# Six of eight output chunks run in pairs, half of their steps with seven block products in place of eight

## The chip, the cores and the metric

The kernel runs on one core of one Trainium2 chip. The metric is device time in microseconds (us) of one execution, the median of three runs. In what follows PE is TensorE with its matmuls, PEld its weight loads (they overlap the matmuls), DVE is VectorE, ACT is ScalarE, POOL is GpSimd and SP the engine that issues the DMAs.

## The reference

One decoder layer with 256 tokens and a width of 4096, all in float32:

```python
proj = einsum('btd,dn->btn', x, w_in)            # 4096 x 12336
q, k_c, v_c, k_s, v_s, k_w, v_w, gates, z_nsa, u, v, z_gm, q_m, z_m = split(proj)
y_nsa = _nsa(q, ..., gates) * silu(z_nsa)        # 16 heads, three branches
y_gm  = _gmlp(u, v, ...) * silu(z_gm)
y_mem = _mem_xattn(q_m, mem, w_mem_kv) * silu(z_m)
h = einsum('btn,nd->btd', concatenate([y_nsa, y_gm, y_mem]), w_out)   # 4096 x 4096
x = layernorm(alpha * x + h, ln_g, ln_b)
```

The change is in the product with `w_out`: 256 rows of y, 4096 deep, 4096 columns.

## The kernel before, in words

**Two-part operands.** PE multiplies float32r operands of 12 significant bits, so every float32 operand is split in two by `split_from` (L184): ACT copies it to a float32r tile (the high half, L185), and DVE subtracts that from the source (the rest, L186). `product3` (L188) then makes three matmuls of 128x128 by 128x512 for one block product: high by rest (L190), rest by high (L191), high by high (L192). The y side is split once; each block of w_out (128 rows by 512 columns) is split when it is needed.

**Chunks and steps.** A chunk is 512 columns of a weight matrix. The eight chunks of `w_out`, `out0` to `out7`, come last. A chunk has 16 steps; a step (`KG = 2`) loads 256 rows of the chunk as one DMA of 512 KB (`load`, three steps ahead, four buffers), splits its two blocks of 128 rows, and multiplies each with both blocks of 128 tokens: 2 x 2 x 3 = 12 matmuls. Two PSUM banks hold a chunk's sums, one for each block of tokens (`c.acc`); five banks are in a ring for this ("acc") and three serve all else ("sd").

**Order.** The program order of each engine is the order of the code. In a step, DVE and ACT split the next step's first block, PE takes this step's first block, and so for the second one. A split has four buffers for its high halves and four for its rests, so ACT starts the high half of a block when PE is done with the block that is four earlier. Work that is not a large product is queued with a delay in steps (`later`), and done by `run_side` at the end of a step.

**What follows a chunk.** `done_out` adds the residual to both sums (`residual`, L794, from PSUM), takes their statistics (L795), and multiplies by the norm's g (L799), spread over three steps of the next chunk. `load_gb` prepares g and b for the final norm in `out2` and `out3`. The last chunk runs its first block of tokens six steps ahead (`LEAD`), and is followed by the norm and the stores.

Of the kernel before, what the change touches and what calls it, by code (L numbers as in the profile page):

```python
# [15 lines left out]
P = 128  # L16
# [34 lines left out]
def decoder_layer(ctx: ExitStack, tc: tile.TileContext, x, mem, w_in, w_cmp_k1, w_cmp_k2, w_cmp_v1,  # L51
# [53 lines left out]
    def warm_up(n):  # L105
        """The tensor engine's clock is at its full rate only after some microseconds of work."""
# [8 lines left out]
    # distance of a query to a key over 256 keys, for the second block of queries; the first  # L115
    # block's is its right half
# [24 lines left out]
    # adds the rows (part, group, chunk) of both parts: chunk j for the first half of block j, and  # L141
    # chunk j + 1 for the second
# [8 lines left out]
    def load_small():  # L151
        """Weights of little size, and their transposes."""
# [29 lines left out]
    # A float32 is the exact sum of its rounding to 12 significant bits and of the rest, which has  # L182
    # 12 bits at most: both are float32r operands of the tensor engine.
# [4 lines left out]
    def product3(out, w, m, start, stop):  # L188
        """w.T @ m of two-part operands, without the product of the two rests (below 2^-24)."""
# [69 lines left out]
    def buffer_T(name):  # L259
        """sums() into one buffer [128, 4, tokens]."""  # L260
# [8 lines left out]
    # -- what becomes of each chunk's result  # L269
# [23 lines left out]
    def add_z(col, dst, name):  # L293
        """z * sigmoid(z) into dst()."""
# [26 lines left out]
    def gated(ps, z, dst, lo_dst, name):  # L321
        """ps * z, in two parts."""
# [16 lines left out]
    def mem_attention(j):  # L339
        """Heads 2j and 2j+1 over the memory tokens."""  # L340
# [154 lines left out]
    # -- keys and values of the selected and the window branch  # L495
# [8 lines left out]
    def keys_cs():  # L504
        """Keys of the groups, transposed: compressed (after a column that is left out), selected."""
# [153 lines left out]
    # -- spatial gating  # L659
# [112 lines left out]
    def load_gb(s):  # L772
        """Rows g, g, b in two parts, the first on partitions 0-2 and the second on 32-34."""
# [16 lines left out]
    def residual(n, i, acc):  # L790
        if n % 4 == 0:
            res[2 * i + n // 4] = page(F32, f"res{i}_{n}")
        r = res_of(i, n)
        nc.vector.scalar_tensor_tensor(r, xr[n][:, i, :], ALPHA, acc, op0=OP.mult, op1=OP.add)  # L794
        nc.vector.bn_stats(fst[:, i, n, :], r)  # L795
# [68 lines left out]
    for n in range(8):  # L864
# [3 lines left out]
    LEAD = 6                    # steps of the last chunk that its first block of tokens is ahead  # L868
# [3 lines left out]
    tail = nsteps - NS          # the first step of the last chunk  # L872
    raw, parts = {}, {}

    def load(i, pieces=1):
        if i >= nsteps:
            return
        c, k = steps[i]
        t = wp.tile([P, KG, 512], F32, name="w", tag="w", bufs=4)
        r0 = c.order[k] * P  # L880
        src = c.w[r0:r0 + KG * P, c.col:c.col + c.width].rearrange("(k p) n -> p k n", p=P)
        for q in range(pieces):
            ks = slice(q * KG // pieces, (q + 1) * KG // pieces)
            nc.sync.dma_start(t[:, ks, :c.width], src[:, ks])
        raw[i] = t

    def split(i, j):
        """The two parts of a step's j-th block of rows."""
        if i >= nsteps:
            return  # L890
        c = steps[i][0]
        kind = "wppywpps"[(i - tail) % 8] if i >= tail else "w"
# [12 lines left out]
        split_from(raw[i][:, j, :c.width], hi[:, :c.width], lo[:, :c.width])  # L905
# [5 lines left out]
    def products_T(i, half):  # L911
        """Blocks 2 * half and 2 * half + 1 of the result's rows."""
# [31 lines left out]
    # prologue  # L944
# [4 lines left out]
    load(0, 2)  # L949
    nc.sync.dma_start(mnat[0][:, :, 256:512], rows0[:, :, 256:512])  # L950
    load(1)
    mnat[1] = load_rows(mem2, 1, "mn")
    load(2)
# [7 lines left out]
    for i in range(tail):  # L961
        now[0] = i
# [4 lines left out]
        load(i + 3)  # L967
        if i < 16 and i % 2 == 0 and i // 2 + 2 < 8:
            mnat[i // 2 + 2] = load_rows(mem2, i // 2 + 2, "mn")
        if c.name.startswith("out") and k == 12:  # L970
# [96 lines left out]
```

## Time and profile before

| | |
|---|---|
| Median of three runs | 1740.77 us (1740.71 to 1741.45) |
| The profiled execution, first to last instruction | 1740.7 us |
| PE busy | 1730.2 us, 99% |
| DVE busy | 1031.7 us, 59% |
| ACT busy | 858.2 us, 49% |
| DMA | 329.03 MB, mean 189 GB/s |
| Mean granted clock of PE | 0.998 |

The profiled execution's span and the median of the runs are the same to 0.1 us, so a sum made against the span stands against the median as well. Durations of matmuls overlap in the records, so the time from one start to the next is what counts for PE.

### The profile page before, as it was taken

What the parts mean: (1) busy time and instruction counts of PE and PEld (TensorE: products, weight loads), DVE (VectorE), ACT (ScalarE), POOL (GpSimd) and SP (SyncE); (2) the same over time, 40 slices, a digit from 0 to 9 for tenths busy, and PEclk for the clock granted to TensorE, in tenths of its full rate; (3) what the DMA queues carried; (4) which work ended last, traced back from release to release, by engine and by line L of the source; (5) the groups of instructions that cost most, each with busy time, mean ns of one, the idle gap of its engine ahead of it and who ended that gap; (6) DMA issues with size and microseconds to landing.
All of it is one profiled execution on the core that took longest, in us unless ns stands there. A gap on an engine that the chain in (4) does not pass through costs nothing.

```text
span 1740.7 us, 24856 instructions
## 1 busy us (share of the span) xinstructions
PE 1730.2 (99%) x9011; PEld 1471.6 (85%) x9011; DVE 1031.7 (59%) x1797; ACT 858.2 (49%) x1592; POOL 6.6 (0%) x18
## 2 busy tenths in 40 slices
PE   9999999999999999999999999999999999999998
PEld 7888888888888899888888888888888888888885
DVE  5555645555665555456676565766655555665565
ACT  4445545454554445445555455655444444554451
POOL 0000000000000000000000000000000000000000
PEclk9999999999999999999999999999999999999999
DMA  7666766655665657665555555556666666666673
GB/s 259 199 186 222 227 187 185 190 158 158 219 215 148 192 165 211 187 184 158 167 158 167 160 147 172 166 169 193 177 193 189 204 210 213 209 214 213 212 230 146
DMA packets 174763, 329.03 MB, mean 189 GB/s; under 512 B 10465, under 2 KB 20005, under 8 KB 174629
## 3 DMA queue, kind: packets, MB, share of 16 engines
q1 hardware_dynamic: 174640, 327.46, 62.6%
q8 instruction: 70, 1.15, 0.3%
q14 instruction: 53, 0.43, 0.1%
HBM read 323.23 MB, written 4.19 MB: 188 GB/s over the span
## 4 chain that ended last, share of the span: by engine, by line
PE 60%; DVE 0%; DVEq 0%; issue 0%; ACT 0%
PE acc L922 13%; PE acc L190 12%; PE acc L192 12%; PE acc L191 12%; PE acc L923 7%; PE ps_pt L631 1%; PE ps_s L584 1%; PE ps_o L190 1%; PE ps_o L192 0%; PE acc L925 0%; PE ps_o L191 0%; PE ps_w L585 0%; DVE res L834 0%; PE ps_s L585 0%; PE ps_ln L830 0%; PE ps_sv L702 0%
## 5 line engine op out<-in xcount | busy, mean ns | idle before, releaser
L186 DVE TENSOR_TENSOR wl<-w,wh 128x512 fp32r<-128x512 f32 (+1 forms) x1160 | 759.6, 677 | 645.8 <-ACT wh L185 639.6
L185 ACT ACTIVATE wh<-w 128x512 fp32r<-128x512 f32 (+1 forms) x1160 | 687.4, 617 | 786.4 <-PE acc L922 362.1
L922 PE MATMUL acc<-x,wh 128*128 128x512 f32 x1984 | 709.6, 400 | 0.5 <-DVE gates L528 0.5
L923 PE MATMUL acc<-x,wl 128*128 128x256 f32 x2048 | 563.3, 280 | 0.1
L922 PEld LDWEIGHTS acc<-x,wh 128*128 128x128 f32 x1984 | 372.8, 188 | 87.6 <-ACT wh L185 2.2
L923 PEld LDWEIGHTS acc<-x,wl 128*128 128x128 f32 x2048 | 386.6, 189 | 7.2 <-DVE wl L186 0.8
L190 PE MATMUL acc<-wl,x 128*128 128x512 f32 (+1 forms) x576 | 215.0, 373 | 0.0
L191 PE MATMUL acc<-wh,x 128*128 128x512 f32 (+1 forms) x576 | 211.8, 368 | 0.0
L192 PE MATMUL acc<-wh,x 128*128 128x512 f32 (+1 forms) x576 | 211.5, 367 | 0.0
L190 PEld LDWEIGHTS acc<-wl,x 128*128 128x128 f32 x576 | 108.2, 188 | 18.1 <-issue 0.9
L192 PEld LDWEIGHTS acc<-wh,x 128*128 128x128 f32 x576 | 108.2, 188 | 17.8
L191 PEld LDWEIGHTS acc<-wh,x 128*128 128x128 f32 x576 | 108.2, 188 | 17.1
L922 PE MATMUL acc<-mem,wh 128*128 128x512 f32 x248 | 90.6, 407 | 0.7 <-DVE mem L186 0.5
L190 PE MATMUL acc<-wl,y_nsa 128*128 128x512 f32 x232 | 90.3, 389 | 0.0
L192 PE MATMUL acc<-wh,y_nsa 128*128 128x512 f32 x232 | 90.3, 389 | 0.0
L191 PE MATMUL acc<-wh,y_nsa 128*128 128x512 f32 x232 | 90.3, 389 | 0.0
L923 PE MATMUL acc<-mem,wl 128*128 128x256 f32 x256 | 71.2, 283 | 0.0
L922 PEld LDWEIGHTS acc<-mem,wh 128*128 128x128 f32 x248 | 47.5, 192 | 12.5 <-DVE mem L186 0.8
L191 PEld LDWEIGHTS acc<-wh,y_nsa 128*128 128x128 f32 x232 | 43.6, 188 | 9.2
L192 PEld LDWEIGHTS acc<-wh,y_nsa 128*128 128x128 f32 x232 | 43.6, 188 | 9.1
L190 PEld LDWEIGHTS acc<-wl,y_nsa 128*128 128x128 f32 x232 | 43.6, 188 | 9.0
L190 PE MATMUL acc<-wl,mem 128*128 128x512 f32 x128 | 51.1, 399 | 0.0
(248 smaller groups left out, 1558.7 us busy)
## 6 DMA issues: line engine op xcount, KB each, us to landing
w<-in_w_in_dram SPq DMA_DIRECT2D x368, 512.0 KB, 3.6
w<-in_w_out_dram SPq DMA_DIRECT2D x128, 512.0 KB, 4.0
w<-in_w_mem_kv_dram SPq DMA_DIRECT2D x63, 512.0 KB, 4.8
w<-in_w_in_dram SPq DMA_DIRECT2D x32, 280.0 KB, 3.2
xn<-in_x_dram SPq DMA_DIRECT2D x8, 512.0 KB, 5.2
xr<-in_x_dram SPq DMA_DIRECT2D x8, 512.0 KB, 5.7
out_dram<-res SPq DMA_DIRECT2D x16, 256.0 KB, 2.0
mn<-in_mem_dram SPq DMA_DIRECT2D x7, 512.0 KB, 5.0
```

Of the source, the lines that this page charges most:

```text
L185: nc.scalar.activation(hi, src, AF.Copy)
L186: nc.vector.tensor_tensor(lo, src, hi.bitcast(F32), op=OP.subtract)
L190: nc.tensor.matmul(out, w[0], m[1], start=start, stop=False)
L191: nc.tensor.matmul(out, w[1], m[0], start=False, stop=False)
L192: nc.tensor.matmul(out, w[0], m[0], start=False, stop=stop)
L584: nc.tensor.matmul(ps[:, :k0], q, keys_cs()[:, g, 1:16 + nk], start=True, stop=True)
L631: nc.tensor.transpose(ps[:n, h * P:(h + 1) * P], src, ident)
L922: nc.tensor.matmul(c.acc[b], hi, x, start=(k + j == 0), stop=False)
L923: nc.tensor.matmul(c.acc[b][:, :SEQ], lo, x[:, :SEQ], start=False, stop=False)
```

## The change

Chunks 0 to 5 of `w_out` run as three pairs (chunks 0 and 1, 2 and 3, 4 and 5); chunks 6 and 7 run as before, after them. Within a pair, a step q covers 256 rows of `w_out` and the columns of both chunks: four blocks of weights B11, B21 (first chunk) and B12, B22 (second chunk), where the first digit is the block of rows; and four blocks A of y, where the first digit is the block of tokens. `KINDS` says how each of the 16 steps runs.

* A step of kind C makes the eight plain block products, 24 matmuls, from four split blocks of weights.
* A step of kind S makes seven block products, 21 matmuls. Its seven operands on the weights' side ("forms") are B11, B21, B22 and four sums: T1 = B12 - B11, T2 = B22 - T1, T3 = B22 - B12, T4 = B21 - T2. Each sum is a DVE operation on 128x512, and is then split by ACT and DVE as a block is. On y's side there are four sums too (`make_sforms`); they are made in the first pair for each of the eight S steps, kept, and used again by the other pairs.

A pair uses all eight PSUM banks, which hold the products P1 to P8; `end_pair` forms the four results from them. There are six buffers for split forms, and `make_form` runs four forms ahead of `use_form`. `load_gb` moves to chunk 6. The core of the diff:

```diff
-    for n in range(8):
+    for n in (6, 7):
         add(w_out, 512 * n, 512, yp, done_out(n), f"out{n}", y_order)
...
+    NPAIR = 3
+    KINDS = "CSCSCSCSCSCSCSSC"
...
+    def make_sforms(q):
...
+        a11, a21, a12, a22 = full[:, 0, :P], full[:, 0, P:], full[:, 1, :P], full[:, 1, P:]
+        nc.vector.tensor_tensor(full, y[:, :, 0].bitcast(F32), y[:, :, 1].bitcast(F32), op=OP.add)
+        nc.vector.tensor_tensor(t[:, 0], a21, a22, op=OP.add)
+        nc.vector.tensor_tensor(t[:, 2], a11, a21, op=OP.subtract)
+        nc.vector.tensor_tensor(t[:, 1], t[:, 0], a11, op=OP.subtract)
+        nc.vector.tensor_tensor(t[:, 3], a12, t[:, 1], op=OP.subtract)
+        split_from(t, sforms[q][:, :, 0], sforms[q][:, :, 1])
...
+            if KINDS[q] == "C":
+                f = [("B11", [("P2", "A11"), ("P4", "A21")]), ("B21", [("P2", "A12"), ("P4", "A22")]),
+                     ("B12", [("P3", "A11"), ("P8", "A21")]), ("B22", [("P3", "A12"), ("P8", "A22")])]
+            else:
+                f = [("B11", [("P1", "A11")]), ("B21", [("P2", "A12")]), ("T1", [("P5", "S1")]),
+                     ("B22", [("P3", "S4")]), ("T2", [("P6", "S2")]), ("T3", [("P7", "S3")]), ("T4", [("P4", "A22")])]
...
+        if j == 0:
+            load_to(min(pbase[s] + 6, len(loads)))
...
+        def summed(a, b2):
+            t = work.tile([P, 512], F32, name="wsum", tag="sm", bufs=5)
+            nc.vector.tensor_tensor(t, a, b2, op=OP.subtract)
+            return t
+        if name[0] == "B":
+            src = b(name)
+        elif name == "T1":
+            src = sums["T1"] = summed(b("B12"), b("B11"))
+        elif name == "T2":
+            src = sums["T2"] = summed(b("B22"), sums["T1"])
+        elif name == "T3":
+            src = summed(b("B22"), b("B12"))
+        else:
+            src = summed(b("B21"), sums["T2"])
+        made[i] = form_slot()
+        split_from(src, *made[i])
...
+        elif what == 1:
+            residual_sum(n0, 0, bk("P2"))
+            residual_sum(n0, 1, bk("P4"))
...
+        elif what == 3:
+            r = res_of(0, n0)
+            nc.vector.tensor_tensor(r, r, sums["U"], op=OP.add)
+            nc.vector.tensor_tensor(sums["U"], sums["U"], bk("P6"), op=OP.add)
...
+    FLEAD = 4
...
+            if m == 0 and j == 0 and q + 1 < NS and KINDS[q + 1] == "S":
+                make_sforms(q + 1)
...
+            make_form(i + FLEAD)
+            use_form(i)
...
+                if j == 3:
+                    end_pair(m, 2)
+                    end_pair(m, 4)
+                    end_pair(m, 5)
+                    for k in range(6, 11):
+                        later(lambda m=m, k=k: end_pair(m, k), k - 5)
```

Before, DVE's row in an output chunk holds only rests, one for each block of weights (`wl`, with `w` the loaded block and `wh` its high half), each of which waits for ACT; here around the end of chunk 0, where the residual (L794), the statistics (L795) and the product with g (L799) stand between the steps:

```order
L186 TENSOR_TENSOR wl<-w,wh 128x512 [waits DMAHW1_49,Activation_49]
L186 TENSOR_TENSOR wl<-w,wh 128x512 [waits Activation_49]
L794 SCALAR_TENSOR_TENSOR res_0_13889<-xr,acc 128x512
L795 BN_STATS fst<-res_0_13889 128x6 [waits DVE_49]
L186 TENSOR_TENSOR wl<-w,wh 128x512 [waits DMAHW2_49,Activation_49]
L186 TENSOR_TENSOR wl<-w,wh 128x512 [waits Activation_49]
```

Now DVE's row in an S step, here one of the second pair: the rests of B11 and B21, then T1 (L1018, `wsum`) and its rest, B22's rest, and T2, T3 and T4, each followed by its rest. The rest of a sum waits for ACT's high half of that sum (`wt` and `wl` are the same kind of buffer in two pools):

```order
L186 TENSOR_TENSOR wl<-w,wh 128x512 [waits DMAHW4_49,Activation_49]
L186 TENSOR_TENSOR wt<-w,wt 128x512 [waits Activation_49]
L1018 TENSOR_TENSOR wsum<-w 128x512 [waits DMAHW5_49]
L186 TENSOR_TENSOR wt<-wsum,wt 128x512 [waits Activation_49]
L186 TENSOR_TENSOR wl<-w,wh 128x512 [waits Activation_49]
L1018 TENSOR_TENSOR wsum<-w,wsum 128x512
L186 TENSOR_TENSOR wl<-wsum,wh 128x512 [waits Activation_49]
L1018 TENSOR_TENSOR wsum<-w 128x512
L186 TENSOR_TENSOR wl<-wsum,wh 128x512 [waits Activation_49]
L1018 TENSOR_TENSOR wsum<-w,wsum 128x512
L186 TENSOR_TENSOR wl<-wsum,wh 128x512 [waits Activation_49]
```

So a step of 11 DVE operations stands where four were; the four rests of the C step follow it.

ACT's row for the same S step and the C step behind it has the high halves in the same order, and those of the four sums now wait for DVE:

```order
L185 ACTIVATE wh<-w 128x512 [waits DMAHW4_49,PE_49,Activation_49]
L185 ACTIVATE wt<-w 128x512 [waits DVE_49,PE_49]
L185 ACTIVATE wt<-wsum 128x512 [waits DVE_49,PE_49,Activation_49]
L185 ACTIVATE wh<-w 128x512 [waits DMAHW5_49,PE_49,Activation_49]
L185 ACTIVATE wh<-wsum 128x512 [waits DVE_49,PE_49,Activation_49] x3
```

So ACT and DVE now wait for each other in turn, four times in an S step.

At the end of a pair DVE's row has, among the rests of the next pair's first forms, 20 operations on 128x512 that make the results; at the end of the first pair they begin like this (L798 is the residual, L1062 to L1076 the sums of `end_pair`):

```order
L798 SCALAR_TENSOR_TENSOR res_0_14386<-xr,acc 128x512
L798 SCALAR_TENSOR_TENSOR res_0_14387<-xr,acc 128x512
L186 TENSOR_TENSOR wl<-w,wh 128x512
L1062 TENSOR_TENSOR res_0_14386<-res_0_14386,u 128x512
L1063 TENSOR_TENSOR u<-u,acc 128x512
L186 TENSOR_TENSOR wl<-w,wh 128x512
L798 SCALAR_TENSOR_TENSOR res_0_14386<-xr,acc 128x512
L798 SCALAR_TENSOR_TENSOR res_0_14387<-xr,acc 128x512
L1066 TENSOR_TENSOR u_14425<-u,acc 128x512
L1067 TENSOR_TENSOR u<-u,acc 128x512
L1070 TENSOR_TENSOR res_0_14387<-res_0_14387,acc 128x512
L1071 TENSOR_TENSOR res_0_14387<-res_0_14387,u 128x512
```

Two stand ahead of the next pair's third form, two ahead of its fourth, and eight ahead of the forms of its first S step; the statistics and the products with g (eight more) follow among that step's forms. Before, four such operations a chunk stood two by two behind a step's rests.

## Rows read from the trace of the kernel before

**Rows 1.** The page's first part: busy time and share of each engine.

```profile
PE 1730.2 (99%) x9011; PEld 1471.6 (85%) x9011; DVE 1031.7 (59%) x1797; ACT 858.2 (49%) x1592; POOL 6.6 (0%) x18
```

**Rows 2.** Stretches of 44 us, output chunks: length, engines' busy time, granted clock, DMA.

```profile
core 0: us, PE busy (x) PEld busy (x) DVE busy (x) ACT busy (x) POOL busy (x), PEclk, DMA share, GB/s
1418.00:1462.00 44.00, 44.00 (x196) 36.45 (x195) 25.76 (x38) 20.71 (x33) 0.00 (x0) 1.00 0.68 210
1636.00:1680.00 44.00, 44.00 (x195) 36.42 (x194) 27.37 (x41) 21.74 (x36) 0.00 (x0) 1.00 0.68 213
```

**Rows 3.** Groups by line and shape, DVE and ACT, 1340 to 1600 us.

```profile
line engine op names shapes xcount | busy us, mean ns | idle before us <-releasers
L186 DVE TENSOR_TENSOR wl<-w,wh 128x512 fp32r<-128x512 f32 x191 | 132.2, 692 | 102.6 <-ACT wh L185 100.6
L799 DVE TENSOR_TENSOR res<-res,gr 128x512 f32<-128x512 f32 x9 | 6.2, 684 | 0.0
...
L185 ACT ACTIVATE wh<-w 128x512 fp32r<-128x512 f32 x191 | 120.8, 632 | 134.8 <-DVE wl L186 117.2 <-PE acc L192 15.4 <-DVE fst L795 2.2
```

**Rows 4.** Timeline of DVE, the residuals of chunk 0 and of chunk 1.

```profile
1418.62 0.69 DVE L186 TENSOR_TENSOR wl<-w,wh 128x512 fp32r<-128x512 f32 x1 [0.67 <-ACT wh L185]
1419.22 0.68 DVE L794 SCALAR_TENSOR_TENSOR res<-xr,acc 128x512 f32<-128x512 f32 x1
1419.94 0.69 DVE L795 BATCH_NORM_STATS2 fst<-res 128x6 f32<-128x512 f32 x1
...
1462.74 0.68 DVE L794 SCALAR_TENSOR_TENSOR res<-xr,acc 128x512 f32<-128x512 f32 x1
```

**Rows 5.** Timeline of DVE where four rests stand behind one another.

```profile
1201.98 2.49 DVE L186 TENSOR_TENSOR wl<-w,wh 128x512 fp32r<-128x512 f32 x4
1204.38 0.22 DVE L688 RECIPROCAL gmmv<-gmmv 128x1 f32<-128x1 f32 x2
```

**Rows 6.** Timeline inside chunk 1: one split, ACT and then DVE.

```profile
1480.51 0.63 ACT L185 ACTIVATE wh<-w 128x512 fp32r<-128x512 f32 x1 [0.73 <-DVE wl L186]
1481.17 0.69 DVE L186 TENSOR_TENSOR wl<-w,wh 128x512 fp32r<-128x512 f32 x1 [0.67 <-ACT wh L185]
...
1485.95 0.63 ACT L185 ACTIVATE wh<-w 128x512 fp32r<-128x512 f32 x1 [0.73 <-PE acc L192]
```

**Rows 7.** Timeline of the last norm, twice: DVE, then ACT on its result.

```profile
1715.94 0.37 DVE L812 BATCH_NORM_AGGREGATE mv<-fst 128x2 f32<-128x48 f32 x1
1716.41 0.30 ACT L813 ACTIVATE mv<-mv,eps 128x1 f32<-128x1 f32 x1 [7.53 <-DVE mv L812]
...
1729.47 0.37 DVE L812 BATCH_NORM_AGGREGATE mv<-fst 128x2 f32<-128x48 f32 x1
1729.88 0.29 ACT L813 ACTIVATE mv<-mv,eps 128x1 f32<-128x1 f32 x1 [11.53 <-DVE mv L812]
```

**Rows 8.** Groups by line and shape, DVE, whole span: other widths.

```profile
L624 DVE TENSOR_SCALAR p<-p,coef 128x128 f32<-128x128 f32 x32 | 6.9, 280 | 0.0
L696 DVE TENSOR_TENSOR vraw<-vraw,gmg 128x1024 f32<-128x1024 f32 x2 | 2.4, 1218 | 0.0
```

**Rows 9.** The page's sixth part: loads of w_out.

```profile
w<-in_w_out_dram SPq DMA_DIRECT2D x128, 512.0 KB, 4.0
```

**Rows 10.** Stretches of 3 us at the end; columns as in rows 2.

```profile
1725.00:1728.00 3.00, 3.00 (x11) 1.42 (x9) 1.73 (x3) 0.00 (x0) 0.00 (x0) 1.00 0.58 225
1728.00:1731.00 3.00, 0.41 (x1) 0.10 (x1) 2.81 (x9) 0.29 (x1) 0.00 (x0) 1.00 0.25 97
1731.00:1734.00 3.00, 2.54 (x6) 1.22 (x6) 2.40 (x5) 0.27 (x1) 0.00 (x0) 0.69 0.25 97
1734.00:1737.00 3.00, 2.53 (x4) 0.90 (x4) 3.00 (x6) 0.00 (x0) 0.00 (x0) 0.50 1.03 398
```

More of the change, by code (lines that the diff above doesn't have):

```diff
@@ L872, in decoder_layer @@
     tail = nsteps - NS
-    raw, parts = {}, {}
-    def load(i, pieces=1):
-        if i >= nsteps:
-            return
[L878 to L885, printed above, removed]
+    first_out = tail - NS
@@ new lines, in decoder_layer @@
+    parts = {}
+    mode = ["in"]
+    NPAIR = 3
+    KINDS = "CSCSCSCSCSCSCSSC"
+    SIDE = [next(q for q in (2 * h, 2 * h + 1) if KINDS[q] == "S") if "S" in KINDS[2 * h:2 * h + 2] else None
+            for h in range(8)]
+    loads, base, pbase = [], {}, {}
+    for i, (c, k) in enumerate(steps):
+        if i == first_out:
+            for m in range(NPAIR):
+                for q in range(NS):
+                    pbase[m * NS + q] = len(loads)
+                    loads += [(w_out, y_order[2 * q] * P, 512 * (2 * m + h), 512) for h in range(2)]
+        base[i] = len(loads)
+        loads.append((c.w, c.order[k] * P, c.col, c.width))
@@ new lines, in decoder_layer, with load_to @@
+    base[nsteps] = len(loads)
+    ntail = base[first_out]
+    raw, loaded = {}, [0]
+    def load_to(n, pieces=1):
+        while loaded[0] < n:
+            i = loaded[0]
+            w, r0, col, width = loads[i]
+            p = i - pbase[0]
+            if 0 <= p < 2 * NPAIR * NS and p // 2 % 3 == 2:
+                if p % 2 == 0:
+                    raw["pg"] = page(F32, "wraw").rearrange("p (h k n) -> p h k n", h=2, k=KG)
+                t = raw["pg"][:, p % 2]
+            else:
+                t = wp.tile([P, KG, 512], F32, name="w", tag="w", bufs=4)
+            src = w[r0:r0 + KG * P, col:col + width].rearrange("(k p) n -> p k n", p=P)
+            for q in range(pieces):
+                ks = slice(q * KG // pieces, (q + 1) * KG // pieces)
+                nc.sync.dma_start(t[:, ks, :width], src[:, ks])
+            raw[i] = t
+            loaded[0] += 1
@@ new lines, in decoder_layer @@
+    sforms = {}
+    def make_sforms(q):
+        b0 = y_order[2 * q]
+        y = yp[b0 // 4].rearrange("p (b s t) -> p b s t", b=4, s=2)[:, b0 % 4:b0 % 4 + 2]
+        if q not in sforms:
+            pg = page(F32R, "sforms").rearrange("p (x f s t) -> p x f s t", x=2, f=4, s=2)
+            free = [p for p in range(NS) if KINDS[p] == "S" and p not in sforms][:2]
+            for x, p in enumerate(free):
+                sforms[p] = pg[:, x]
+        full = work.tile([P, 512], F32, name="yfull", tag="y").rearrange("p (k t) -> p k t", k=2)
+        t = work.tile([P, 512], F32, name="ysum", tag="y").rearrange("p (f t) -> p f t", f=4)
+        a11, a21, a12, a22 = full[:, 0, :P], full[:, 0, P:], full[:, 1, :P], full[:, 1, P:]
[5 more added lines that the diff above has]
+        split_from(t, sforms[q][:, :, 0], sforms[q][:, :, 1])
@@ new lines, in decoder_layer, with before_pair, __init__ @@
+    pxr, pgr = {}, {}
+    def before_pair(m):
+        pxr[m] = page(F32, "xr").rearrange("p (h t d) -> p h t d", h=2, t=NT)
+        g = work.tile([P, NT, 512], F32, name="gr", tag="nat")
+        for h in range(2):
+            n = 2 * m + h
+            nc.sync.dma_start(pxr[m][:, h], x2[:, n * 512:(n + 1) * 512].rearrange("(t p) d -> p t d", p=P))
+            nc.sync.dma_start(g[:, h], bcast_rows(ln_g[n * 512:(n + 1) * 512], 512))
+            xr[n], gr[n] = pxr[m][:, h], g[:, h]
+    class Form:
+        def __init__(self, make, uses):
+            self.make, self.uses, self.parts = make, uses, None
@@ new lines, in decoder_layer @@
+    forms = []
+    nuse = {}
+    for m in range(NPAIR):
+        for q in range(NS):
+            s = m * NS + q
+            if KINDS[q] == "C":
[4 more added lines that the diff above has]
+                     ("B22", [("P3", "S4")]), ("T2", [("P6", "S2")]), ("T3", [("P7", "S3")]), ("T4", [("P4", "A22")])]
+            for j, (name, uses) in enumerate(f):
+                forms.append((m, q, j, len(f), name, uses))
+                for bank, _ in uses:
+                    nuse[m, bank] = nuse.get((m, bank), 0) + 1
@@ new lines, in decoder_layer, with make_form @@
+    made, sums, used = {}, {}, {}
+    def make_form(i):
+        if i >= len(forms):
+            i -= len(forms)
+            if i < KG:
+                split(first_out, i)
+            return
+        m, q, j, n, name, uses = forms[i]
+        s = m * NS + q
+        if j == 0:
+            load_to(min(pbase[s] + 6, len(loads)))
+        b = lambda x: raw[pbase[s] + int(x[2]) - 1][:, int(x[1]) - 1]
+        def summed(a, b2):
[10 more added lines that the diff above has]
+            src = summed(b("B22"), b("B12"))
+        else:
+            src = summed(b("B21"), sums["T2"])
+        made[i] = form_slot()
+        split_from(src, *made[i])
@@ new lines, in use_form @@
+    def use_form(i):
+        m, q, j, n, name, uses = forms[i]
+        for bank, f in uses:
+            k = used.get((m, bank), 0)
+            if k == 0:
+                banks[m, bank] = psum.tile([P, 512], F32, name="acc", tag=ROLE_TAG[bank],
+                                           bufs={"acc": 5, "sd": 3}[ROLE_TAG[bank]])
+            product3(banks[m, bank], [a_op(q, f, p) for p in range(2)], made[i], k == 0, k == nuse[m, bank] - 1)
+            used[m, bank] = k + 1
+        del made[i]
@@ L891, in split @@
         c = steps[i][0]
+        if i == first_out and mode[0] != "out":
+            return
         kind = "wppywpps"[(i - tail) % 8] if i >= tail else "w"
@@ L959, in decoder_layer, with step @@
     split(0, 1)
-    for i in range(tail):
-        now[0] = i
+    def step(i):
+        now[0] += 1
         c, k = steps[i]
@@ L977, in decoder_layer @@
         products(i, 0)
-        if not c.sums:
+        if last_in:
+            make_form(1)
+        elif not c.sums:
             split(i + 1, 1)
@@ L997, in decoder_layer @@
         run_side()
+    now[0] = -1
+    for i in range(first_out):
+        step(i)
+    mode[0] = "out"
+    run_pairs()
+    for i in range(first_out, tail):
+        step(i)
     c = chunks[-1]
```

97 lines of the change are left out of this document (85 added, 12 removed).

## The prediction

> **What bounds the kernel now.** I read the page's first part, then the stretches of the output chunks, then the timeline inside a chunk. PE is busy for 99% of the span [rows 1]. In an output chunk it is busy for 44.00 of 44 us at a granted clock of 1.00, the level of 2.4 GHz, while DVE works 25.8 and ACT 20.7 us [rows 2]. So PE sets the pace, and DVE has some 18 us in 44 to give. The residual of chunk 1 starts 43.52 us after that of chunk 0 [rows 4]; a chunk has 16 steps of 12 matmuls, so a step takes 2.72 us and a matmul 0.2267 us. DVE and ACT wait in every split [rows 3, 6], but that is slack: ACT's high half waits for a buffer that PE frees, DVE's rest waits for the high half, and PE never waits for the rest.
>
> **What the change takes from PE.** Each S step saves 3 of 24 matmuls: 24 S steps, 72 matmuls, 16.3 us. An S step then needs 21 x 0.2267 = 4.76 us of PE and a C step 5.44, together 10.20, where the same work took 10.88. This is the gain if PE stays the bound.
>
> **What it asks of DVE.** Prices first. A rest on 128x512 lasts 0.69 us [rows 3], but four in a row start 2.40 us apart in all [rows 5], so one costs 0.60 when it need not wait. If it needs the result of the operation before it on DVE, it starts 0.72 us after that one's start, 0.04 after its end [rows 4]. A sum of two blocks is not in the trace; the nearest row is the product with g, also two float32 tensors of 128x512, with 0.684 [rows 3], so I take the same 0.69 and 0.60. Nothing lower has a row.
>
> A sum must be split, and the order's rows show that nothing stands between a sum and its rest on DVE, which works in order. ACT started 0.10 and 0.04 us after the end of the DVE operation whose result it needed [rows 7]; I take 0.07. The high half lasts 0.63, and DVE starts 0.03 after it [rows 6]. So a summed form costs DVE 0.69 + 0.07 + 0.63 + 0.03 = 1.42 until its rest starts, and 0.60 for the rest: **2.02 us**, of which 0.73 are spent waiting for ACT.
>
> An S step has three plain forms and four sums: 3 x 0.60 + 4 x 2.02 = 9.88 us. A C step has four plain forms: 2.40. Together **12.28 us, against 10.20 that PE needs and 10.88 before.** So DVE becomes the bound, and PE waits for forms in the S steps. The six buffers don't add a wait: DVE has a C step's four forms done in 2.40 us, makes B11 and B21 of the S step in the two buffers left (3.60), and T1's high half needs the buffer of the C step's first form, which PE has left 1.36 us after it got it. Nor do they help: a lead of six forms is used up once, and the shortfall returns with each S step. 24 such pairs of steps are 294.7 us.
>
> **The rest that now lies on DVE's path.** It lay beside PE before.
> - The sums of y, eight times in the first pair. One addition on 512 columns, then four on 128, then a split. The rows at 512 and 1024 columns [rows 3, 8] are 0.53 us apart, so 128 columns take 0.40 less than 512: 0.29 long, 0.20 apart, which the operation on 128x128 at 0.28 bears out [rows 8]. Starts: 0; 0.73 (it waits for the first); 0.93; 1.13; 1.46 (it waits for the third to end at 1.42); the end at 1.75, 0.07 to ACT, 0.63, 0.03: the rest at 2.48, the next operation at 3.08. 8 x 3.08 = 24.6 us.
> - The end of a pair: 20 operations (four residuals, eight additions, four statistics, four products with g), of which one waits for the one before: 12.1 us, and some 0.2 until PE is done with P2 and P4. Twice, 24.7 us. At the third end only 12 of them stand ahead of chunk 6's second step: 7.5 us; the other eight fall into chunk 6, two to a step, where a step's two rests and two of these need 2.4 of 2.72 us, and cost nothing.
> - What follows the last input chunk (two products, two rests of y_gm): 4 x 0.60 = 2.4 us.
> - The first matmul of chunk 6's second step waits 0.73 us for its rest.
> - To be taken off: the first four forms are still made at PE's old pace, the fourth rest ending the sum's 2.40 us when PE is 1.26 us into chunk 0, so DVE's path begins 1.1 us ahead of PE's.
>
> Sum from PE's start of chunk 0 to chunk 6's second step: 294.7 + 24.6 + 24.7 + 7.5 + 2.4 + 0.7 - 1.1 = **353.5 us**. Before, this stretch took 6 x 43.52 + 2.72 = 263.8. The difference is 89.7 us, and 1740.7 + 89.7 = **1830 us**. The profiled span and the median of the runs agree, so nothing is added for what lies around.
>
> **Edits that cost nothing.** ACT has 11 high halves of 0.63 = 6.9 us in 12.28. The loads of w_out are as many as before; those of a step are asked for when its second predecessor begins, some 12 us ahead, and land in 4.0 [rows 9]; without that cover each S step could wait up to 4.0. The g and b rows of the last norm move to chunks 6 and 7: eight operations on DVE and on ACT, 4.8 us in some 16 us of slack a chunk [rows 2]; without slack 4.8.
>
> **A rule of the skill against a row.** Rows 5 show a DVE operation starting 0.60 us after one that lasts 0.69. The Trainium skill's page "VectorE: DVE Perf Modes", section "The DRAIN you can't avoid", says that the next operation does not start until the pipe is empty. By the rule each would cost its full 0.69; by the row it doesn't, and the row has four cases. I take the row. If sums and rests in turn went at 0.69 (the first rival below), 11 operations in each pair of steps and 52 at the pairs' ends would cost 0.09 more each, with 0.7 in the sums of y: 29 us, and 1859.
>
> **The rivals.**
> 1. *DVE at full length, 0.69 for each operation.* For it: an operation that needs the one before takes 0.72 [rows 4], and T2 and T4 read earlier sums. Against: those sums are two and more operations old. 1859 us.
> 2. *PE's clock falls.* With DVE as the bound PE stands idle in each S step; most in the first pair, where it works 10.2 of 15.4 us. For it: at the end of the kernel, after a stretch with 0.41 us of matmuls in 3, the granted clock fell to 0.69 and then 0.50 [rows 10], the level of 1.2 GHz, and stayed there through a stretch with four matmuls in 3 us. Against: the gaps here are 2.02 - 0.68 = 1.3 us within a step, and longer only at the start of a pair; and while the sums of y make DVE slow, PE has slack to work slowly in. If the first pair's 360 matmuls ran at the lower level they would take 163 us, where DVE needs 8 x 15.36 + 2.4 = 125: 38 us more, 1868. If all 1080 of the pairs did, 490 us in place of 353.5: 1967. The Trainium skill's page "TensorE: Matmul & The Clock Gate", section "A second HAM failure mode: psum-queue depth-cycling", tells of short idle times between groups of matmuls that made the clock swing between the two levels; no run of before shows that.
> 3. *PE stays the bound, and the kernel is faster.* The mechanism is that DVE's wait for ACT is filled and its other work fits beside PE; then the 16.3 us are a gain, 1724.4. The point from which it decides: of the 263.8 us that the stretch took, the sums of y, pairs' ends and the rest take 58.8, so 205.0 are left, 8.54 for an S and a C step with 15 operations. That is 0.57 each with no wait at all. The rows have 0.60, and the order shows no operation to fill the four waits. With no wait DVE would need 9.00 us and PE's 10.20 would hold in the second and third pair, 81.6 us each; the first would take 8 x (9.00 + 3.08 - 0.73) + 2.4 = 93.2. That is 256.4, or 7.4 less than before, 1733; but the pairs' ends, 32 us where nothing hides them, make a loss of it unless three quarters of them lie beside PE.
>
> **Chances and numbers.** My forecast has 0.70, the full length 0.08, the clock 0.12, PE as the bound 0.05; 0.05 stay for what I don't see. A measurement of this kernel can tell about 0.2%, 3.5 us, from no change. Within my forecast the hand-over at 0.04 or 0.10 moves 96 sums by 2.9 us either way, and 0.72 in place of 0.60 at every sum would add 96 x 0.12 = 11.5; its own range is 1818 to 1848. With the rivals at 1859 and 1868 it reaches to 1865 at the top; 1810 at the bottom takes in some waits for ACT that are shorter than I count (0.2 us in each of 96). Faster has 0.03, no change 0.02, slower 0.95.
>
> **What the profile after would show.** DVE busy near all the time in the pairs but for waits on ACT's `wh` and `wt` at L186, 0.7 us each and 96 of them; S and C together near 15.4 us in the first pair and 12.3 in the others; PE's idle time there 353.5 - 1080 x 0.2267 = 109 us, ended by DVE's rests; an L1018 at 0.68. A granted clock under 0.95 in the pairs would speak for the second rival; L186 starting 0.69 apart with no wait for the first. A PE that is still 99% busy in the second pair would make the prediction wrong, and so would a wait of DVE on ACT much under 0.7.

## The result and the profile after

Four runs of each kernel give a median of 1845.61 us (1844.85 to 1846.31) against 1741.11 (1740.71 to 1743.21); the ratio of the runs is **1.0598, 95% interval 1.0583 to 1.0613.** The forecast was 1830 with a range of 1810 to 1865. The profiled execution has a span of 1844.1 us, and its device time is 1845.82: in this and every later run that has both, the time lies some 1.7 us above the span.

The page's first part, where [rows 1] has PE at 99% and DVE at 59%:

```profile
PE 1761.3 (96%) x8939; PEld 1470.2 (80%) x8939; DVE 1157.6 (63%) x2037; ACT 892.6 (48%) x1675; POOL 6.6 (0%) x18
```

PE has 72 matmuls fewer and the kernel takes longer, and no engine is full: the share over the whole span does not name the bound. The stretches of the three pairs do (length, then the engines' busy time, granted clock, DMA), read against [rows 2]:

```profile
core 0: us, PE busy (x) PEld busy (x) DVE busy (x) ACT busy (x) POOL busy (x), PEclk, DMA share, GB/s
1377.00:1510.00 133.00, 104.23 (x366) 76.33 (x365) 98.82 (x177) 57.54 (x101) 0.00 (x0) 0.86 0.44 140
1510.00:1622.00 112.00, 91.99 (x358) 68.19 (x357) 86.25 (x139) 50.30 (x89) 0.00 (x0) 0.95 0.50 162
1622.00:1735.00 113.00, 92.82 (x362) 68.59 (x361) 87.52 (x141) 49.03 (x87) 3.60 (x2) 0.95 0.48 156
```

PE is idle for 20 to 29 us in each pair, and DVE, the forecast bound, for 25 to 34. (PE's three sum to 69, where 109 were forecast: at a lower granted clock its matmuls last longer and fill part of the gaps.) What DVE's idle time is shows in its timeline, here an S step of the second pair and the C step behind it, and in ACT's for the same sums (start, length, idle time before and its releaser in brackets):

```profile
1557.27 0.68 DVE L1018 TENSOR_TENSOR wsum<-wraw 128x512 f32<-128x512 f32 x1
1558.73 0.69 DVE L186 TENSOR_TENSOR wl<-wsum,wh 128x512 fp32r<-128x512 f32 x1 [0.78 <-ACT wh L185]
1559.34 0.68 DVE L186 TENSOR_TENSOR wl<-wraw,wh 128x512 fp32r<-128x512 f32 x1
1559.94 0.68 DVE L1018 TENSOR_TENSOR wsum<-wraw,wsum 128x512 f32<-128x512 f32 x1
1561.41 0.69 DVE L186 TENSOR_TENSOR wl<-wsum,wh 128x512 fp32r<-128x512 f32 x1 [0.78 <-ACT wh L185]
...
1566.44 2.49 DVE L186 TENSOR_TENSOR wl<-w,wh 128x512 fp32r<-128x512 f32 x4
```

```profile
1558.07 0.63 ACT L185 ACTIVATE wh<-wsum 128x512 fp32r<-128x512 f32 x1 [1.93 <-DVE wsum L1018]
...
1560.74 0.63 ACT L185 ACTIVATE wh<-wsum 128x512 fp32r<-128x512 f32 x1 [1.52 <-DVE wsum L1018]
```

One sum is a relay. DVE ends T1 at 1557.27 + 0.68 = 1557.95; ACT starts 0.12 later, at 1558.07, and ends at 1558.70; DVE starts the rest at 1558.73, 0.03 later. In between DVE stands still for 0.78 us, since its next instruction in order is that rest. ACT in turn waits for the next sum. 93 of the 96 rests behind a sum wait 0.78. From T1 of one S step to T1 of the next, with a C step between them, DVE takes 12.51 us in most steps of the second and third pair (12.28 forecast) and 15.55 in most of the first (15.36), as in these two rows of it:

```profile
1430.43 0.68 DVE L1018 TENSOR_TENSOR wsum<-w 128x512 f32<-128x512 f32 x1
...
1445.98 0.69 DVE L1018 TENSOR_TENSOR wsum<-w 128x512 f32<-128x512 f32 x1
```

The groups of the stretch 1374 to 1740 us, for the sizes:

```profile
L186 DVE TENSOR_TENSOR wl<-wsum,wh 128x512 fp32r<-128x512 f32 x64 | 44.3, 692 | 50.2 <-ACT wh L185 50.2
L185 ACT ACTIVATE wh<-wsum 128x512 fp32r<-128x512 f32 x64 | 40.4, 631 | 112.7 <-DVE wsum L1018 108.2 <-PE acc L192 4.5
L190 PE MATMUL acc<-wl,sforms 128*128 128x512 f32 x64 | 28.4, 444 | 24.8 <-DVE wl L186 20.5 <-DVE y_gm L186 4.3
```

The three rows read as one chain: ACT waits for DVE's sum, DVE for ACT's high half (50.2 us in 64), PE for DVE's rest. In [rows 3] DVE and ACT wait in every split too, but there PE is busy for 44.00 of 44 us [rows 2].

### The profile page after: what moved, and what is told of

Read it like the earlier page. It is cut to its first block, busy times and chain, and to the rows that moved or that the text cites. A ratio compares the mean times of both kernels' runs of the same rounds, so it can differ in the third digit from the quotient of the medians.

```text
span 1844.1 us, 25064 instructions
## 1 busy us (share of the span) xinstructions
PE 1761.3 (96%) x8939; PEld 1470.2 (80%) x8939; DVE 1157.6 (63%) x2037; ACT 892.6 (48%) x1675; POOL 6.6 (0%) x18
## 4 chain that ended last, share of the span: by engine, by line
PE 42%; DVE 14%; ACT 4%; issue 2%; ACTq 0%; DMA 0%; DVEq 0%; SPq 0%
PE acc L1153 13%; PE acc L190 7%; PE acc L1154 6%; PE acc L191 6%; PE acc L192 6%; DVE wl L186 6%; ACT wh L185 3%; DVE wsum L1018 3%; DVE wt L186 2%; ACT wt L185 1%; PE ps_pt L631 1%; PE ps_s L584 1%; PE ps_o L190 0%; PE acc L1156 0%; PE ps_o L192 0%
## 5 line engine op out<-in xcount | busy, mean ns | idle before, releaser
L186 DVE TENSOR_TENSOR wl<-w,wh 128x512 fp32r<-128x512 f32 (+1 forms) x1045 | 676.7, 674 | 539.5 <-ACT wh L185 535.6
L185 ACT ACTIVATE wh<-w 128x512 fp32r<-128x512 f32 (+1 forms) x1045 | 610.5, 614 | 661.8 <-PE acc L1153 362.6
L185 ACT ACTIVATE wh<-wsum 128x512 fp32r<-128x512 f32 x64 | 40.4, 631 | 112.7 <-DVE wsum L1018 108.2
L186 DVE TENSOR_TENSOR wl<-wsum,wh 128x512 fp32r<-128x512 f32 x64 | 44.3, 692 | 50.2 <-ACT wh L185 50.2
L190 PE MATMUL acc<-wl,y_nsa 128*128 128x512 f32 x128 | 53.3, 416 | 8.2 <-DVE wl L186 8.2
L192 PE MATMUL acc<-wh,y_nsa 128*128 128x512 f32 x128 | 52.3, 409 | 0.0
L191 PE MATMUL acc<-wh,y_nsa 128*128 128x512 f32 x128 | 52.2, 408 | 0.0
L190 PE MATMUL acc<-wl,sforms 128*128 128x512 f32 x64 | 28.4, 444 | 24.8 <-DVE wl L186 20.5
```

The source lines that it names most:

```text
L185: nc.scalar.activation(hi, src, AF.Copy)
L186: nc.vector.tensor_tensor(lo, src, hi.bitcast(F32), op=OP.subtract)
L190: nc.tensor.matmul(out, w[0], m[1], start=start, stop=False)
L191: nc.tensor.matmul(out, w[1], m[0], start=False, stop=False)
L192: nc.tensor.matmul(out, w[0], m[0], start=False, stop=stop)
```

## The experiments

All times are medians. Those of the kernel before lay between 1741.4 and 1743.0 on the chips used, and each ratio is that of the record, against the runs on its own chip; it can differ from the quotient of two medians in the fourth digit.

**All blocks of C.** No sum, no seven products; pairs, six buffers, `end_pair`'s four residuals and the moved loads stay.

```diff
+    KP = ["C" * 16] * 3
-            if KINDS[q] == "C":
+            if KP[m][q] == "C":
...
-            if m == 0 and j == 0 and q + 1 < NS and KINDS[q + 1] == "S":
+            if False:
```

> All 16 steps of every pair are of kind C: pairs, eight-bank code, six form buffers, loads and chunk order as in the change, but no S step, no sums of weights, no sums of y and no additions at a pair's end. Theory (in S steps DVE and ACT hand each sum back and forth, and DVE becomes the bound; sums of y and pair ends come on top): nothing of that is left, DVE needs 4.8 us in the 10.9 that PE takes for two steps, so the time is that of the kernel before, 1741, at most 4 more for the ends of the pairs. Rival (the pairing itself costs: banks that wait for the sums of the pair before, or loads of two chunks at a time): 1750 or more.

Measured: 1744.24 us, 1.0018 (1.0008 to 1.0027). So the pairs as such, and with them the lead of four forms and the g and b rows in chunk 6, cost about 3 us. The other 101 us come from the S steps and what they bring: sums of weights and of y, the additions at a pair's end, and the four banks that C steps leave unused.

**Sums made ahead.** The same operations; DVE makes each sum two forms before its split, so that plain rests stand between a sum and its own rest.

```diff
+            make_sum(i + FLEAD + 2)
             make_form(i + FLEAD)
             use_form(i)
...
-        elif name == "T1":
-            src = sums["T1"] = summed(b("B12"), b("B11"))
...
+        src = b(name) if name[0] == "B" else presum.pop(i)
```

> As the change, but each sum of weights is issued two forms earlier than its split, so that other DVE work stands between a sum and its rest; the same operations in number and kind. Theory: DVE's four waits of 0.78 us in an S step vanish, DVE needs 15 x 0.60 = 9.0 us for an S and a C step and PE's 10.2 hold in pairs two and three; the first pair stays DVE-bound at 11.4 with its sums of y. 93.6 + 2 x 81.6 + some 13 for the pairs' ends = 270 in place of 365: about 1748, between 1742 and 1765. Rival (DVE's number of operations is what costs, or operations at full length): little changes, 1815 or more. Rival (PE's clock is what costs): 1810 or more.

Measured: 1766.44 us, 1.0142 (1.0126 to 1.0157): 79 of the 104 us are gone, with as many operations on DVE (2037) and matmuls (8939) as before the edit; the time is a little above the range. DVE's timeline of an S step in the third pair:

```profile
1585.35 0.69 DVE L1014 TENSOR_TENSOR wsum<-wraw 128x512 f32<-128x512 f32 x1
...
1594.39 0.68 DVE L1014 TENSOR_TENSOR wsum<-w 128x512 f32<-128x512 f32 x1
1594.99 1.29 DVE L186 TENSOR_TENSOR wt<-w,wt 128x512 fp32r<-128x512 f32 x2
1596.20 0.69 DVE L1014 TENSOR_TENSOR wsum<-w,wsum 128x512 f32<-128x512 f32 x1
1596.80 0.69 DVE L186 TENSOR_TENSOR wl<-wsum,wh 128x512 fp32r<-128x512 f32 x1
1597.40 0.69 DVE L1014 TENSOR_TENSOR wsum<-w 128x512 f32<-128x512 f32 x1
1598.00 0.69 DVE L186 TENSOR_TENSOR wl<-w,wh 128x512 fp32r<-128x512 f32 x1
```

The operations start 0.60 apart, with no bracket behind any. From T1 to T1 an S and a C step take 9.03 us while PE is behind, which is the third rival's 15 x 0.60, and 10.33 once PE is the bound. Where the rest of the loss lies can be read from PE's starts. Before, two chunks took PE 88.0, 87.0 and 87.0 us. Here the three pairs take 104.4, 90.2 and 89.7, where PE alone would need 8 x 10.33 = 82.6. The first pair, whose steps DVE holds at 12.08 (9.03 and 3.05 for the sums of y), is 16.4 longer than before; the others save 4.4 each on PE, lose 7 to 7.5 around the pairs' ends, and are 3.1 and 2.6 longer. Chunk 6's first two steps are 2.8 longer. That is 24.9 us, and 25.0 lie between the medians.

**First pair of C.** Its sums of y are still made there; the other pairs are as changed.

```diff
+    KP = ["C" * 16, KINDS, KINDS]
-            if KINDS[q] == "C":
+            if KP[m][q] == "C":
```

> The first pair runs all its steps as kind C but still makes the sums of y beside them; pairs two and three as in the change. Theory: in the first pair DVE needs 4.8 + 3.1 us in the 10.9 of PE, so PE is the bound again there, 87 us in place of 127, and its end has eight operations fewer: about 1792 (1785 to 1800). Rival (the sums of y are hidden already and the S steps alone cost): the first pair gains only 8 x 1.6 = 13 us: about 1832. Rival (the clock): if most of the excess was the first pair's clock, the rest of the excess would go with it: under 1775.

Measured: 1799.96 us, 1.0326 (1.0308 to 1.0343). That is at the top of the range. The S steps of one pair, the one with the sums of y, were worth 46 us, and the interval in the other two stayed at 12.51.

**PE kept busy.** Products with a block of zeros are added behind those of the sums: five each in the first pair and two in the others, then two everywhere. They fill PE's idle time and add zero. (A bank's last product has none behind it, so they are 261 and 174 in all, not the 288 of the expectation.)

```diff
+            if name[0] == "T" and k < nuse[m, bank] - 1:
+                for _ in range(5 if m == 0 else 2):
+                    nc.tensor.matmul(banks[m, bank], zr, made[i][0], start=False, stop=False)
```

> As the change, with matmuls of a zero block added behind the products of each sum (five in the first pair, two in the others, into the bank just used, so the sums are unchanged), to keep PE at work while DVE and ACT make the next form. Theory (DVE is the bound, the lower clock a small extra where PE is late): the granted clock in the pairs rises towards 1.00 and the time falls by 3 to 8 us, 1837 to 1843, though PE does 24 x 12 more matmuls. Rival (the clock is the main cost): it falls by 30 us or more. Rival (PE is the bound): it rises by 0.2267 x 288 = 65 us.

> As the change, with two matmuls of a zero block behind the products of each sum in every pair (five in the first pair before, which made PE late at that pair's end). Theory (the low clock costs only where DVE must wait for PE at a pair's end): the steady steps stay at 15.55 and 12.51 us, the first pair's end goes from 25.9 towards 23.6, and the time is 1838 to 1844. Rival (the low clock costs nothing at all): 1845 as before. Rival (the clock is a main cost): under 1830.

Measured: 1846.32 us, 1.0600 (1.0585 to 1.0616), with up to five; 1846.83, 1.0595 (1.0577 to 1.0614), with two. The first two pairs' stretches with up to five:

```profile
1377.00:1510.00 133.00, 124.14 (x514) 98.31 (x515) 98.60 (x174) 56.28 (x98) 0.00 (x0) 0.96 0.41 140
1510.00:1622.00 112.00, 101.49 (x405) 77.28 (x405) 84.25 (x136) 49.99 (x89) 0.00 (x0) 0.95 0.49 163
```

PE takes 29 x 5 = 145 matmuls more in the first pair, the granted clock there rises from 0.86 to 0.96, DVE's busy time is the same, and so is the kernel's time. PE is not the bound, since a PE that was would have taken the fillers' time in full. The gain of a few us that both expectations had did not come. In the steps a higher clock changes little: from T1 to T1 most still take 15.56 and 12.51, and three slower ones in the kernel as changed (16.41, 13.03 and 13.04) fall to 15.64, 12.51 and 12.51, which is 1.8 us, while the first one grows by 0.7. But the fillers are themselves in the way at the pairs' ends, where DVE needs PE's banks: with up to five the first end, from T1 to T1, goes from 25.92 to 27.04 and the second from 23.68 to 26.36, and with two to 25.40 and 26.19. So these runs show that the clock is not the main cost; they do not show that it costs nothing, and what it costs at the ends they do not separate.

**A lead of five forms** in place of four (`FLEAD = 5`).

> As the change, with forms made five ahead of their use in place of four, the most that six buffers allow. Theory: a lead is used up once and the shortfall of 2.3 us returns with each pair of steps, so the time stays at 1845, within 4 us. Rival (PE stalls because the lead is too short for the longer S step): 1815 or less.

Measured: 1848.43 us, 1.0606 (1.0588 to 1.0625). The six buffers and the lead are not what DVE waits for.

**Both cures, and then the pairs' ends spread.** Sums ahead and the first pair of C; and then, with it, two additions of a pair's end moved ahead of its last matmuls, and the last ten of its 20 operations spread over the first steps of the next pair.

```diff
-                    for k in range(6, 11):
-                        later(lambda m=m, k=k: end_pair(m, k), k - 5)
+                    for k, d in zip(range(6, 11), (1, 2, 3, 4, 5) if m == NPAIR - 1 else (2, 6, 7, 10, 11)):
+                        later(lambda m=m, k=k: end_pair(m, k), d)
```

> Sums of weights issued two forms ahead, and the first pair all of kind C with the sums of y beside it. Theory: PE is the bound in the first pair (87 us) and in the steady part of the other two (10.2 to 10.3 us for an S and a C step); what stays is some 9 us at each of two pair ends, against 16 x 0.68 = 10.9 us saved on PE: 1746, between 1740 and 1752. Rival (S steps cost PE time for another reason, so that a kernel with them stays slower): 1755 or more.

> As the run with the sums ahead and the first pair all C, and the ends of the pairs spread: two of the additions move ahead of the pair's last matmuls, and the additions that free no bank, the statistics and the products with g of the first two pairs are delayed into the C steps of the next pair. Theory (the pair ends' 20 DVE operations make PE wait at the next pair's first S step): half or more of the 9 us at each end goes, 1738, between 1732 and 1744, at or a little below the kernel before. Rival (banks that come free late at a pair's end are what costs there): no better than the run it is made from.

Measured: 1753.15 us, 1.0059 (1.0044 to 1.0073), and 1749.79, 1.0042 (1.0029 to 1.0054). The direction held and the size did not: the first is 1 us over its range, the second 6. PE's steps took 10.33 where 45 x 0.2267 = 10.20 were counted on, which is 2 us in 16 of them and led to the next run. More is lost elsewhere: with the ends spread PE still takes 92.1 us for the first pair, 3 more than with all blocks of C, 6.0 more than its 82.6 for the third, and 4.5 more than before for chunk 6's first two steps.

**Four buffers.** All C as in the first experiment, with the four buffers of the kernel before and a lead of three.

```diff
-        if f < 4:
+        if True:
...
-    FLEAD = 4
+    FLEAD = 3
```

> Pairs with all steps of kind C, as in the first run, but with the four split buffers of the kernel before in place of six, and a lead of three forms in place of four. In the pairs of every run so far a matmul starts 0.2296 us after the one before it, where it was 0.2267 before; 1152 matmuls make 3.3 us of that, as much as the first run stood above the kernel before. If the two added buffers (from another pool) are the cause, the pitch returns to 0.2267 and the time to 1741. If they are not (four banks in use in turn, loads into other places), it stays at 0.2296 and 1744.

Measured: 1741.62 us, 0.9998 (0.9989 to 1.0007). The 3 us of the first experiment go with the two added buffers (`wt`); the lead was changed along with them, but the slower starts are those of the matmuls on `wt`. PE's timeline of the first experiment, with six buffers, where 12 matmuls on `wt`, 24 on `wl` and `wh`, and 12 on `wt` follow one another:

```profile
1559.58 0.39 PE L190 MATMUL acc<-wt,y_mem 128*128 128x512 f32 x1
...
1562.38 0.39 PE L190 MATMUL acc<-wl,y_mem 128*128 128x512 f32 x1
...
1567.84 0.39 PE L190 MATMUL acc<-wt,y_mem 128*128 128x512 f32 x1
...
1570.63 0.39 PE L190 MATMUL acc<-wl,y_nsa 128*128 128x512 f32 x1
```

The 12 on `wt` take 2.80 us, 0.2333 each; the 24 on the others 5.46, 0.2275. With four buffers twelve take 2.72, as before:

```profile
1560.02 0.39 PE L190 MATMUL acc<-wl,y_mem 128*128 128x512 f32 x1
...
1562.74 0.39 PE L190 MATMUL acc<-wl,y_mem 128*128 128x512 f32 x1
```

Over 1152 matmuls of three all-C pairs, 8.26 in place of 8.16 us for 36 is 3.2 us.

**Fewer S steps.** Six in a pair, in the second and third pair alone, with sums ahead and ends spread, the sums of y at the third form of a step; first with six buffers, then with four, a lead of three, and the last pair's end spread over chunk 6.

```diff
-    KINDS = "CSCSCSCSCSCSCSSC"
+    KINDS = "CCSCSCSCSCSCSCCC"
+    KP = ["C" * 16, KINDS, KINDS]
```

> As the run with spread ends, with six S steps in each of the last two pairs in place of eight, none within two steps of a pair's start or end, and the sums of y made two forms later in a step, so that they no longer stand ahead of the operation that frees the last input chunk's bank (PE waited 2.9 us for it). Theory: every wait of PE on DVE in the pairs goes but for about 1 us; 1116 matmuls at 0.2296 are 256.2 us against 261.2 before: 1737, between 1735 and 1741. Rival (something else than DVE's lateness costs at the ends): 1745 or more.

> As the run with six S steps, with the four split buffers of the kernel before and a lead of three forms, the last pair's end spread over chunk 6 (two DVE operations to a step), and the statistics and products with g of the other pairs put into C steps. Theory: the matmul pitch is back at 0.2267, PE waits for DVE some 2 to 3 us in all, and 36 matmuls are saved, 8.2 us: 1736, between 1733 and 1739, faster than both kernels. Rival (with four buffers DVE cannot run ahead far enough for an S step): 1742 or more.

Measured: 1745.04 us, 1.0017 (1.0008 to 1.0026; one of its 11 executions took 3458 us, is not in the ratio, and is not explained), and 1743.61, 1.0012 (1.0003 to 1.0021). Both missed: neither beats the kernel before. The saving of 12 S steps is 36 x 0.2267 = 8.2 us; where it goes in the second of them shows in PE's timeline in the third pair:

```profile
1572.41 0.39 PE L192 MATMUL acc<-wh,y_nsa 128*128 128x512 f32 x1
1572.76 0.50 PE L190 MATMUL acc<-wl,sforms 128*128 128x512 f32 x1
1573.09 0.40 PE L191 MATMUL acc<-wh,sforms 128*128 128x512 f32 x1
1573.33 0.40 PE L192 MATMUL acc<-wh,sforms 128*128 128x512 f32 x1
1573.96 0.50 PE L190 MATMUL acc<-wl,sforms 128*128 128x512 f32 x1 [0.24 <-DVE wl L186]
1574.30 0.40 PE L191 MATMUL acc<-wh,sforms 128*128 128x512 f32 x1
```

A plain block feeds PE for 6 matmuls, 1.36 us, a form of an S step for 3, 0.68, and DVE needs 1.20 for a summed form. A form that comes late delays its matmul, and the one behind it starts 0.34 later and not 0.23: the printed wait of 0.24 costs 0.63 + 0.34 - 2 x 0.2267 = 0.52. Starts over 0.25 apart add up to 3.5 us over the normal pace in the second pair and 5.4 in the third, 8.9 in all, against 8.2 saved. So the form that comes late takes the saving back.

**Sums on POOL.** As sums ahead with the first pair of C (1753.15), but POOL, idle in the pairs, makes the sums, three forms ahead.

```diff
-        nc.vector.tensor_tensor(t, b(u), b(v) if v[0] == "B" else sums[v], op=OP.subtract)
+        nc.gpsimd.tensor_tensor(t, b(u), b(v) if v[0] == "B" else sums[v], op=OP.subtract)
...
-            make_sum(i + FLEAD + 2)
+            make_sum(i + FLEAD + 3)
```

> As e6_ahead_first_c (1753), but the 64 sums of blocks of the second and third pair are made by POOL, three forms ahead, and DVE keeps the rests. If DVE's count of operations is what still holds PE up there, DVE's share of an S and a C step falls from 15 x 0.60 = 9.0 us to 11 x 0.60 = 6.6, PE sets the pace with 45 matmuls x 0.2296 = 10.33 in every pair of steps, the ends of the pairs lie beside it, and the time is 1745 (1741 to 1749), near but not under the kernel before. The rival: POOL is too slow, or POOL and DVE hold each other up. No run here has POOL's time for two blocks; from 10.33 / 4 = 2.58 us for one sum on, POOL sets the pace, and if DVE's rests stand still while POOL works, 4 sums and 11 rests share 10.33 us, which ends at 0.93 us for a sum: then the time lies above 1753, with ACT waiting for POOL's sums and rests that last longer than 0.69.

Measured: 1769.3 us, 1.0156 (1.0139 to 1.0173), 16 us more than with the sums on DVE: the rival. The timelines of POOL and of DVE; the last four sums and DVE's rows are of the same stretch:

```profile
1570.97 10.13 POOL L1015 TENSOR_TENSOR wsum<-wraw 128x512 f32<-128x512 f32 x1 [0.71 <-DVE wt L186]
...
1594.68 1.46 POOL L1015 TENSOR_TENSOR wsum<-w 128x512 f32<-128x512 f32 x1 [5.47 <-DMA w<-in_w_out_dram]
1596.23 1.63 POOL L1015 TENSOR_TENSOR wsum<-w,wsum 128x512 f32<-128x512 f32 x1
1597.82 1.76 POOL L1015 TENSOR_TENSOR wsum<-w 128x512 f32<-128x512 f32 x1
1599.55 1.75 POOL L1015 TENSOR_TENSOR wsum<-w,wsum 128x512 f32<-128x512 f32 x1
```

```profile
1594.93 1.77 DVE L186 TENSOR_TENSOR wt<-wraw,wt 128x512 fp32r<-128x512 f32 x1
1596.62 5.23 DVE L186 TENSOR_TENSOR wl<-wraw,wh 128x512 fp32r<-128x512 f32 x3
1601.77 0.68 DVE L186 TENSOR_TENSOR wl<-w,wh 128x512 fp32r<-128x512 f32 x1
```

While POOL makes four sums, DVE makes four rests in 1594.93 to 1601.77, 1.71 each where they take 0.60 alone; as soon as POOL is done they are back at 0.60. The other way round, one of POOL's sums, begun at 1570.97, lasted 10.13 us, and DVE worked without a break up to 1579.92. How long POOL takes for a sum alone no run shows. The Trainium skill's page "SBUF — State Buffer", section "SBUF: two separate sides", states that DVE and GpSimd share one pair of ports as an exclusive lock, also where a DVE operation has two inputs in SBUF and the GpSimd operation reads SBUF. The rows agree: rests and sums both have their inputs there, and each engine's operations last longer while the other works.

## Why the prediction was right, and where its sizes were off

**DVE becomes the bound: shown.** Taking its wait away without taking an operation (sums ahead) gave 79 of 104 us back; giving PE 261 more matmuls, or one more form of lead, left the time within 3 us. What bounds is DVE's path of work and waits, and not DVE's work alone: it is busy for 273 of 358 us in the pairs. All C steps, which have no relay, brought the loss down to 3 us.

**A sum costs a relay of 2.02 us: right in kind, 2.07 measured.** The step that was mis-sized is the hand-over from DVE to ACT. We took 0.07 between the 0.10 and 0.04 of [rows 7], two operations on 128x2; at the sums of 128x512 it is 0.12, above both rows. The rest of the term held: 0.68 for a sum whose price was taken from the product with g in [rows 3], 0.63 for the high half, 0.03 back, 0.60 for the rest. 96 sums by 0.05 are 4.8 us.

**The sums of y: right.** From the first addition at 1375.99 to the next rest at 1379.04 are 3.05 us, 3.08 forecast.

**The pairs' ends: 2.2 us short at the first.** From T1 to T1 the first end takes 25.92 us and the second 23.68. The two residuals on P2 and P4 waited at the first 1.97 us for PE, which ran at a granted clock of 0.57 from 1498 to 1506; we had counted PE as done 0.2 us after DVE.

```profile
1504.79 1.49 DVE L798 SCALAR_TENSOR_TENSOR res<-xr,acc 128x512 f32<-128x512 f32 x2 [1.97 <-PE acc L192]
```

```profile
1498.00:1506.00 8.00, 6.90 (x19) 5.42 (x19) 5.41 (x9) 5.13 (x10) 0.00 (x0) 0.57 0.49 159
```

**What the sum left out.** The stretch from PE's start of chunk 0 (1374.52) to chunk 6's second step (1739.42) is 364.9 us, 353.5 forecast. Of the 11.4 between them 4.8 are the hand-over, 2.2 the first pair's end, and 2.4 are six single waits of DVE for ACT beyond the usual ones, 0.06 to 0.78 each, in all three pairs. Another 1.2 are the two rests of chunk 6's first step, which stand on DVE between the last C step and the operations of the third end, and which the sum had at nothing; 0.8 are not assigned.

**The time before was taken too short.** The forecast counts 6 x 43.52 + 2.72 = 263.8 us for this stretch in the kernel before; its trace has 264.8, since chunk 0 took 44.49. So the stretch grew by 100.1 us. PE reaches it 1.3 later, which is within the scatter: in the traces of the other runs chunk 0 starts between 1371.3 and 1375.5. Chunk 6's second step takes 4.45 in place of 2.72, 1.7 more, most of it at a granted clock of 0.50 (1740.5 to 1743.5), and 0.4 come after it. That makes up the 103.4 between the two spans. The other 1.1 of the 104.5 between the medians lies between spans and times: a span of 1740.7 and a median of 1740.77 were taken as the same, but every later run of that kernel has a time some 1.7 above its span.

**Edits that cost nothing: nearly so.** With the added buffers PE's matmuls start further apart (0.2295 on average in pairs of C steps, 0.2267 without). That is 3 us where PE sets the pace, and does not enter where DVE does.

**Rival 1, DVE at 0.69 an operation: refuted.** Sums and rests in turn start 0.60 apart. The section "The DRAIN you can't avoid" of the Trainium skill's page "VectorE: DVE Perf Modes", which the prediction set against its row, goes on to say that a next operation that is not held starts earlier. The rows agree with that.

**Rival 2, PE's clock: its sign came, its price did not.** The clock was 0.86 in the first pair, under the 0.95 that we had named as speaking for it, and 0.95 in the others, and in one stretch of 4 us (1394 to 1398) it was 0.50, the level of 1.2 GHz. But lifting the first pair's to 0.96 left the time as it was, so the 38 us of this rival are refuted. Where DVE had to wait for PE it did cost something: at the first pair's end (part of the 2.2 us), in chunk 6's second step (1.7), and in single waits (1.8 went with the fillers), a few us in all. The sign was a poor one, since in most steps PE had time to work slowly in.

**Rival 3, PE stays the bound: refuted as the code stands, half right once the sums are ahead.** Its 9.00 us for 15 operations were met (9.03). Its 1733 us were not within reach: the wait inside the sums of y stays (3.05 each, not 2.35), the pairs' ends lie on the path, and PE's pace is 10.33.

## What to carry to other kernels

Before trading matmuls for sums, price the engine that prepares the operands: here three matmuls less (0.68 us of PE) were bought with eleven DVE operations in place of four, 4.2 us more at best and 7.7 as the code was written (3 x 0.60 + 4 x 2.07 - 2.40). Where one in-order engine hands a tile to another and needs it back for its very next instruction, it stands still for the whole round trip; the producing operation belongs some instructions ahead of the use. An idle engine is not always a place for work: POOL had nothing to do, and its sums held up DVE's rests.

## What the runs showed of the hardware that was not expected

* Matmuls whose 512-column operand lies in the two added buffers start 0.2333 us apart, those on the four old ones 0.2275 in the same steps and 0.2267 when the two are not there. The difference goes when they are taken away (with the lead cut from four to three in the same run); whether it is their place in memory or something else stays open, and no run tells that.
* In the run with four buffers and six S steps a matmul that waited is followed by the next one after 0.33 to 0.34 us, not 0.23, so that the printed wait of 0.24 cost 0.52.
* Sums of two tensors on POOL took 1.30 us at the least, 1.75 in the median and 10.13 at the most, and held DVE's rests at 1.71 each meanwhile.
* In the first pair the clock swung between its two levels while PE was idle for 22% of the time, with little cost to the kernel, since DVE set the pace.
